# Fifteen pairs of a Strassen feed-forward block: seven wide quarter products into two-bank accumulators

## The chip, the cores and the metric

The kernel runs on one core of a Trainium2 chip. The core has a matrix engine (TensorE; PE in the profile, with its weight loads as PEld), a vector engine (VectorE, DVE), a scalar engine (ScalarE, ACT), GpSimd (POOL) and SyncE (SP), which here only issues DMAs. Each engine works through its own queue in order. TensorE writes its results to an accumulator memory, PSUM, of eight banks; one bank holds 512 float32 values in each of 128 partitions. The metric is the device time of one execution in microseconds (us), lower is better.

## The reference, cut to what matters

One layer of a streaming encoder: a feed-forward half step, a mixer of convolution and gated linear attention, a second feed-forward half step, an embedding gate, a final norm. 512 tokens, model width 1024, feed-forward width 2816, all in float32.

```python
def _swiglu(x, w_in, w_out):
    gate, up = jnp.split(x @ w_in, 2, axis=-1)
    return (jax.nn.silu(gate) * up) @ w_out
...
        h = h + 0.5 * _swiglu(_rmsnorm(h, ffn1_norm[i]), ffn1_w_in[i], ffn1_w_out[i])
        z = _rmsnorm(h, mix_norm[i]) @ w_in[i]
...
        h = h + jnp.concatenate([y_conv, y_gla], axis=-1) @ w_out[i]
        h = h + 0.5 * _swiglu(_rmsnorm(h, ffn2_norm[i]), ffn2_w_in[i], ffn2_w_out[i])
        gate = jax.nn.sigmoid(_rmsnorm(h, ple_norm[i]) @ ple_w_gate[i])
        h = h + gate * (p[i] @ ple_w_proj[i])
    return _rmsnorm(h, final_norm)
```

## The kernel before

Activations lie transposed: features on the 128 partitions, the 512 tokens along the free axis. Every operand of TensorE is split into a high and a low part (ACT rounds the high part, DVE subtracts it from the original to get the low part), and a product is the sum of three: high by high, high by low, low by high.

The first product of each feed-forward block is done in eleven **pairs**: pair i takes 256 gate columns and the 256 matching up columns of w_in. A pair is a 2 by 2 block product in the form of Strassen and Winograd: seven quarter products in place of eight. `m1` to `m7` in `ffn` are the seven; each multiplies a quarter of the weights (512 by 256, named a11, a12, a22, s1 to s4) with a quarter of the activations (512 by 256 tokens, b11, b21, b22, t1 to t4). A few pairs at the start (pairs 0 and 1 in the first block, pair 0 in the second) are done plainly, without the seven products.

There are two forms of a quarter product, both over four blocks of 128 rows and two blocks of 128 columns:

- `mul` (line 341): for each row and column block three matrix instructions of 256 columns, 24 in all, into one bank (two halves of 256).
- `mul2` (line 357): for each row and column block one instruction of 512 columns, which takes the weight's high part against the high and the low half of the activations side by side, and then one of 256 columns for the weight's low part: 8 and 8, 16 in all, into two banks (a tile `pd`). The sum of the two 256-column halves is left to DVE.

Before the change m7 and m4 use `mul2`; m1, m2, m6, m5 and m3 use `mul`. One accumulator, p.x, is shared by m1, m6, m5 and m3, and ACT copies its state out (`snap`) after each of the first three; p.y holds m2; p.w holds m7 and m4. `plus` (line 687) adds an accumulator and a copy on DVE and multiplies by the row scale.

The second product (by w_out) runs in pieces of 48 instructions for a group of two pairs (`second`, line 822); a piece writes two banks, and DVE adds them to the residual h. Two pieces come with each pair. The list `units` sets the order on TensorE; in a steady stretch it is m6, m7, m5 of pair i, m1, m2 of pair i+1, a piece, m4, m3 of pair i, a piece. `drive` makes the weights' parts four units ahead of their use (`AHEAD`), fetches seven to nine ahead, and runs what a unit leaves over (`left`) around the next unit. The wrapper `Ordered` pins the order of PE, DVE and ACT to the order in which the program issues.

Weights come in 512 KB transfers on SP's queue into six raw buffers (`wr`); the high and low parts have six buffers each (`wh`, `wl`).

PSUM before: five single banks and one `aux` bank in a pool that is open all the time, and two more banks that are either one two-bank tile (`bank2`, p.w) or two single banks (`spare`).

After the second block comes the embedding gate stage (from line 1610), one Strassen product of its own, whose order on ACT and DVE is mostly left to the scheduler.

Of the kernel before, what the change touches and what calls it, by code (L numbers as in the profile page):

```python
# [62 lines left out]
def block_kernel(ctx: ExitStack, tc: tile.TileContext, a: dict, out: bass.AP):  # L63
# [12 lines left out]
    pp = ctx.enter_context(tc.tile_pool(name="ps", bufs=8, space=PSUM))  # L76
# [30 lines left out]
    wide, turn_no, narrow_only = [None, None], [0], [True]  # L107

    def region(double):
        if wide[0] != double:  # L110
            if wide[1] is not None:
                wide[1].close()
            wide[:] = double, ExitStack()
            wide.append(wide[1].enter_context(tc.tile_pool(name=nm("pw"), bufs=1, space=PSUM)))
        return wide[-1]

    def bank2():
        return region(True).tile([P, 2, SEQ], F32, tag="mm2", bufs=1, name=nm("pd"))

    def spare():  # L120
        return region(False).tile([P, SEQ], F32, tag="mm", bufs=2, name=nm("ps"))

    def bank():
        turn_no[0] += 1
        if not narrow_only[0] and turn_no[0] % 7 in (5, 6):
            return spare()
        return pp.tile([P, SEQ], F32, tag="mm", bufs=5, name=nm("ps"))

    def aux():
        return pp.tile([P, SEQ], F32, tag="aux", bufs=1, name=nm("ax"))  # L130

# [187 lines left out]
    class Norm:  # L319
# [5 lines left out]
        def add(self, h):  # L325
            if self.n == 0:
                act.activation(self.acc, h, AF.Square)
            else:
                sq = tmp("sq", bufs=3)
# [11 lines left out]
    def mul(ps, w, x, first, last, ks=range(4)):  # L341

        (wh, wl), k0 = w, ks[0]
        for k in ks:
            xh, xl = x[k]
# [11 lines left out]
    def mul2(ps, w, x, first, last):  # L357

        wh, wl = w
        at = [(k, i, slice(i * P, (i + 1) * P)) for k in range(4) for i in range(2)]  # L360
        for k, i, cs in at:
            pe.matmul(two(ps[:, i]), wh[:, k, cs], x[k][0], start=(first and k == 0), stop=False, skip_group_check=True)
        for k, i, cs in at:
            pe.matmul(ps[:, i, 0:HALF], wl[:, k, cs], x[k][1], start=False, stop=last and k == 3, skip_group_check=True)
# [6 lines left out]
    class Right:  # L371
# [3 lines left out]
        def __init__(self, rows, gname):  # L375
            self.rows, self.gname = rows, gname
            self.raw, self.op = {}, {}
            for k in range(2):
                for half in range(2):
                    hs = slice(half * HALF, (half + 1) * HALF)  # L380
                    self.op[f"b{k + 1}{half + 1}"] = [tuple(t[:, hs] for t in rows[4 * k + c]) for c in range(4)]
# [20 lines left out]
        def split(self, *names):  # L402
            for name in names:
                op = self.op[name] = []
                for jp in range(2):
                    src = self.raw.pop((*T_KEYS[name], jp))
                    if name == "t4":
                        for jj in range(2):
                            hi, lo = self.op["b12"][2 * jp + jj]
                            act.copy(hi, src[:, jj])  # L410
                            sub(lo, src[:, jj], hi.bitcast(F32))
                            op.append((whole_of[id(self.rows[2 * jp + jj][0])][1][:, :, HALF:], hi))
# [5 lines left out]
                    if name == "t3":  # L418
                        whole = whole_of[id(pair_[0])][1]
                        op += [(whole[:, :, jj * HALF:(jj + 1) * HALF], hi[:, jj]) for jj in range(2)]  # L420
                    else:
                        op += [(hi[:, jj], lo[:, jj]) for jj in range(2)]
# [100 lines left out]
    def square_x(i):  # L523

        tile_, t0, nt = squares[i]
        sq = tmp("sq", bufs=3).rearrange("p (t c) -> p t c", t=nt)
# [55 lines left out]
    ps0 = [bank(), bank(), spare(), spare()]  # L582
# [79 lines left out]
    def ffn(w_in, w_out, x, gname, given, first, rsb, hooks, plain, far={}, casts={}, adds=()):  # L662
# [9 lines left out]
        pairs = {i: given.get(i) or Left(w_in, 2 * i) for i in range(npair)}  # L672

# [13 lines left out]
        def plus(ps, t, i, name):  # L687
            o = tmp(name)
            if len(ps.shape) == 3:
# [17 lines left out]
        def snap(ps, name, **kw):  # L707
            o = tmp(name, **kw)
# [13 lines left out]
        def m1(p):  # L722
            p.x = bank()
            mul(p.x, p.part("a11"), x.op["b11"], True, False)
            p.a = snap(p.x, "sq", bufs=3)

        def m2(p):
            p.y = bank()
            mul(p.y, p.part("a12"), x.op["b21"], True, True)
# [4 lines left out]
            if p is pairs[start]:  # L734
                after["m7" if plain else "m5", start] = [gate0] if plain else [lambda: pairs[start + 1].cast("s1", "s3"), gate0]
                return []
            return [gate0]

        def m6(p):
            mul(p.x, p.part("s2"), x.op["t2"], False, False)  # L740
            p.u2 = snap(p.x, "u2", bufs=1)

        def m7(p):
            p.w = bank2()
            mul2(p.w, p.part("s3"), x.op["t3"], True, False)

        def m5(p):
            mul(p.x, p.part("s1"), x.op["t1"], False, False)
            p.u = plus(p.w, snap(p.x, "sq", bufs=3), 1, "u1")
# [13 lines left out]
        def plain_unit(j):  # L763

            up, i, k = j // 4, j // 2 % 2, j % 2
            def run(p):
                if not j:
                    p.g, p.s = {}, {}
                if not k:
                    p.x = bank()  # L770
# [53 lines left out]
        def second(cut):  # L824
# [7 lines left out]
            def piece(n, g, begin, final, key=None):  # L832
# [7 lines left out]
                def run():  # L840
                    left = []
                    wh, wl = got.pop((f0, n, g))
                    for i in range(2):
                        if begin:
                            ps[n + i] = (spare if last and n == 4 else bank)()
# [6 lines left out]
                        if final:  # L852
                            h = hT[n + i]
                            dve.scalar_tensor_tensor(out=h, in0=ps[n + i], scalar=0.5, in1=h,
                                                     op0=ALU.mult, op1=ALU.add)
                            if last:
                                hi, lo = bt2(s="hg")
                                act.activation(hi, h, AF.Copy, scale=vec(gname, n + i))
                                left.append((h, hi, lo, vec(gname, n + i)))
# [42 lines left out]
        for i in range(start, npair):  # L902
            add("m6", i)
# [5 lines left out]
            else:  # L909
# [26 lines left out]
        narrow_only[0], turn_no[0] = False, 0  # L936
# [17 lines left out]
    hooks.update({("m5", 3): lambda *_: made[0](), ("m5", 4): lambda *_: constants(),  # L954
# [288 lines left out]
    def outputs(t2):  # L1243
# [13 lines left out]
        for t in (2 * t2, 2 * t2 + 1):  # L1257
            junk = tmp("sq", bufs=3)
# [239 lines left out]
    narrow_only[0] = True  # L1498

    def plain_block(p, up, i, mid={}):  # L1500
        ps = (spare if i else bank)()
# [34 lines left out]
    hooks.update({("m7", 10): lambda *_: turn_p(0), ("m5", 10): lambda *_: turn_p(1)})  # L1536
# [129 lines left out]
    def inputs(t, e, spare=False):  # L1666
# [3 lines left out]
        pq, pt = bank(), aux() if spare else bank()  # L1670
# [89 lines left out]
    def kept(ps, name, **kw):  # L1760
        o = tmp(name, **kw)
# [16 lines left out]
    x_, y_ = [bank(), bank()], [bank(), bank()]  # L1778
# [8 lines left out]
    m1 = [kept(p_, "sq", bufs=3) for p_ in x_]  # L1787
# [24 lines left out]
    w_ = [bank(), bank()]  # L1812
# [9 lines left out]
    x5 = [kept(p_, "sq", bufs=3) for p_ in x_]  # L1822
# [7 lines left out]
    b22 = [added(high(t)) for t in q22]  # L1830
# [36 lines left out]
    wide[1].close()  # L1867
# [23 lines left out]
```

## Time and profile before

| | |
|---|---|
| Time, median of 3 runs | 941.72 us (941.43 to 942.06) |
| The profiled execution | 941.44 us |
| Its span, first to last instruction | 939.7 us |
| VectorE busy, share of the span | 785.9 us, 84% |
| ScalarE busy | 483.1 us, 51% |
| GpSimd busy | 55.9 us, 6% |
| Granted TensorE clock, mean | 0.997 |

A row of the profile gives an engine, an operation, output and inputs by the program's tile names, a count, the busy time and the mean duration. Nearly all instructions are recorded through one helper, so their line is always L46, and one tells them apart by tiles: `hg` are the normalized activations, `t` their sums, `act` the input of the second product, `wr` raw weights, `wh` and `wl` their parts, `ps` single banks, `pd` two-bank tiles, `sq` and `u` the copies of accumulators, `g` a gate value, `h` the residual.

### The profile page before, as it was taken

How to read it: one execution, taken by the hardware profiler on the slowest of the kernel's cores; microseconds unless marked ns; L12 is line 12 of the kernel's file. 1: busy time of each engine (PE TensorE's matmuls, PEld its weight loads, DVE VectorE, ACT ScalarE, POOL GpSimd, SP SyncE). 2: the span in 40 equal slices, each digit the busy share in tenths (PEclk: the TensorE clock that was granted, in tenths of full speed). 3: DMA queues.
4: the chain of work that ended last, by engine and by line, in shares of the span. 5: the costliest groups of instructions: out<-in, count | busy, mean ns of one | idle time of the engine just before them, and what ended most of it. 6: DMA issues, size and time to landing. Idle time of an engine off the chain costs nothing.

```text
span 939.7 us, 14172 instructions
## 1 busy us (share of the span) xinstructions
PE 929.2 (99%) x5611; PEld 816.8 (87%) x5611; DVE 785.9 (84%) x1077; ACT 483.1 (51%) x730; POOL 55.9 (6%) x74
## 2 busy tenths in 40 slices
PE   9999999999999999999999999999999999999996
PEld 7898999899989988788877889999899999998875
DVE  6798987898789676999986789988888888876986
ACT  5874444344444474463564875444434433446873
POOL 0100000000000111001120020000000000000130
PEclk9999999999999999999999999999999999999998
DMA  7633332342223593256552563432243224347463
GB/s 228 189 107 114 113 107 88 101 135 90 90 91 112 147 261 86 68 126 144 136 134 75 150 150 97 132 104 79 91 135 112 68 90 135 105 160 208 90 109 115
DMA packets 108134, 114.45 MB, mean 122 GB/s; under 512 B 5203, under 2 KB 96517, under 8 KB 108068
## 3 DMA queue, kind: packets, MB, share of 16 engines
q1 hardware_dynamic: 101748, 94.67, 32.8%
q0 software_dynamic: 6304, 18.88, 11.0%
q8 instruction: 44, 0.72, 0.3%
q14 instruction: 22, 0.18, 0.1%
q10 hardware_dynamic: 16, 0.00, 0.0%
HBM read 93.61 MB, written 2.10 MB: 102 GB/s over the span
## 4 chain that ended last, share of the span: by engine, by line
PE 97%; DMA 1%; ACT 1%; DVE 1%; issue 0%; POOLq 0%; ACTq 0%; DVEq 0%
PE ps L46 84%; PE pd L46 11%; PE ax L46 1%; DMA sm<-in_ple_w_gate 1%; ACT s L46 0%; DVE s L46 0%; ACT wh L46 0%; ACT wl L46 0%; ACT sq L46 0%; DVE u L46 0%; DVE rs L46 0%; ACT yc L46 0%; DVE y L46 0%; DVE g L46 0%; DVE lnsq L46 0%
## 5 line engine op out<-in xcount | busy, mean ns | idle before, releaser
L46 PE MATMUL ps<-hg,wh 128*128 128x256 f32 (+1 forms) x1232 | 262.2, 312 | 0.1
L46 DVE TENSOR_TENSOR wl<-wr,wh 128x1024 fp32r<-128x1024 f32 (+2 forms) x161 | 188.1, 1179 | 37.7 <-ACT wh L46 37.6
L46 PEld LDWEIGHTS ps<-hg,wh 128*128 128x128 f32 x1232 | 201.7, 191 | 14.1 <-issue 1.3
L46 ACT CAST wh<-wr 128x1024 fp32r<-128x1024 f32 (+2 forms) x178 | 177.6, 1020 | 50.1 <-DMA wr<-in_ffn_w_out 27.4
L46 PE MATMUL ps<-hg,wl 128*128 128x256 f32 (+1 forms) x616 | 187.6, 311 | 0.0
L46 PE MATMUL ps<-act,wh 128*128 128x512 f32 x512 | 158.0, 390 | 0.0
L46 ACT ACTIVATE s<-g 128x512 f32<-128x512 f32 x48 | 30.4, 633 | 191.2 <-DVE g L46 191.2
L46 PEld LDWEIGHTS ps<-hg,wl 128*128 128x128 f32 x616 | 117.6, 191 | 6.4
L46 PEld LDWEIGHTS ps<-act,wh 128*128 128x128 f32 x512 | 95.1, 188 | 19.0
L46 PE MATMUL ps<-t,wh 128*128 128x256 f32 x608 | 111.0, 283 | 0.0
L46 PE MATMUL ps<-act,wl 128*128 128x512 f32 x256 | 99.6, 389 | 0.0
L46 PEld LDWEIGHTS ps<-t,wh 128*128 128x128 f32 x608 | 95.9, 192 | 1.2
L46 PE MATMUL ps<-t,wl 128*128 128x256 f32 x304 | 86.1, 283 | 0.0
L46 DVE SCALAR_TENSOR_TENSOR cv<-glu,cw,cv 128x502 f32<-128x502 f32 (+24 forms) x90 | 61.8, 729 | 0.3
L46 DVE TENSOR_TENSOR wl<-sm,wh 128x1024 fp32r<-128x1024 f32 x42 | 51.2, 1221 | 8.8 <-ACT wh L46 8.8
L46 PEld LDWEIGHTS ps<-t,wl 128*128 128x128 f32 x304 | 58.3, 192 | 0.0
L46 PEld LDWEIGHTS ps<-act,wl 128*128 128x128 f32 x256 | 48.1, 188 | 10.1
L46 PE MATMUL ps<-wh,hg 128*128 128x512 f32 x176 | 54.8, 393 | 0.1
L46 DVE SCALAR_TENSOR_TENSOR h<-ps,h 128x512 f32<-128x512 f32 x80 | 51.7, 682 | 2.3 <-PE ps L46 2.2
L46 ACT COPY sq<-ps 128x512 f32<-128x512 f32 x42 | 24.4, 584 | 55.9 <-PE ps L46 55.7
L46 ACT CAST wh<-sm 128x1024 fp32r<-128x1024 f32 x42 | 43.8, 1043 | 5.3 <-DMA sm<-in_ple_w_gate 2.9
L46 DVE TENSOR_TENSOR u<-pd,u 128x512 f32<-128x512 f32 x57 | 39.3, 689 | 5.9 <-PE pd L46 4.6
(307 smaller groups left out, 1501.5 us busy)
## 6 DMA issues: line engine op xcount, KB each, us to landing
wr<-in_ffn_w_in SPq DMA_DIRECT2D x84, 512.0 KB
wr<-in_ffn_w_out SPq DMA_DIRECT2D x32, 512.0 KB
wr<-in_w_in SPq DMA_DIRECT2D x20, 512.0 KB
wl<-wr POOLq DMA_DIRECT2D x18, 512.0 KB, 5.3
wr<-in_ffn_w_out SPq DMA_DIRECT2D x16, 384.0 KB
wr<-in_w_out SPq DMA_DIRECT2D x8, 512.0 KB
wq<-in_ple_w_gate SPq DMA_DIRECT2D x8, 512.0 KB
wl<-wq POOLq DMA_DIRECT2D x8, 512.0 KB, 4.9
```

Source lines behind the costliest of these rows:

```text
L46: inst = call(*args, **kwargs)
```

## The change

All later pairs (from the second pair after the first Strassen pair on: pairs 4 to 10 of the first block, 3 to 10 of the second, fifteen in all) do all seven products with `mul2` into two-bank accumulators. What follows from that is changed along with it.

- PSUM is laid out per stage. Two banks (`fixed`) are always open. With them goes either `singles` (three banks and `aux`, and two banks that are `spare` or one `double(True)`), or, while `mode` is 2, `doubles` (two two-bank tiles for p.x and p.y, and one for p.w).
- p.x and p.y are two-bank tiles; which of the two is taken first alternates from pair to pair, so that m1 writes the one that held p.y of the pair before.
- The pairs come one behind the other: m1, m2, m6, m7, m5, piece, m4, m3, piece, all of pair i. The pieces write the two `fixed` banks.
- ACT copies 1024 values a partition instead of 512 out of p.x (two buffers `sq` of 1024 in place of three of 512). `plus` on a two-bank tile and a two-bank copy adds 1024 values, then the two halves, then multiplies by the row scale. m3's result is copied by halves and summed.
- The gate after m2 is summed behind m7 and goes through silu behind m5; m3's silu runs ahead of the piece behind it.
- In the last group, pieces n = 2 and 4 write two-bank tiles, and their two additions to h wait for both products.
- In the embedding gate stage the accumulators are `spare` and `fixed` banks, and the rounding of q22 is put behind the copies `x5`.

```diff
+    def fixed():
+        return psum(region("fixed"), 2, [P, SEQ])
...
+    def double(last=False):
+        kind = ("fixed", "doubles" if mode[0] == 2 else "singles", "double")
+        return psum(region(*kind) if last else region(*kind[:2]), 1 if last else 2, [P, 2, SEQ])
...
     def mul2(ps, w, x, first, last):
+        if len(ps.shape) == 2:
+            return mul(ps, w, x, first, last)
...
-            pe.matmul(two(ps[:, i]), wh[:, k, cs], x[k][0], start=(first and k == 0), stop=False, skip_group_check=True)
+            pe.matmul(two(ps[:, i]), wh[:, k, cs], x[k][2], start=(first and k == 0), stop=False, skip_group_check=True)
...
+        for i, p in pairs.items():
+            p.wide = start + 2 <= i
...
         def plus(ps, t, i, name):
...
             else:
-                dve.tensor_tensor(out=o, in0=ps, in1=t, op=ALU.add)
+                dve.tensor_tensor(out=t, in0=ps, in1=t, op=ALU.add)
+                dve.tensor_tensor(out=two(o), in0=t[:, :, 0:HALF], in1=t[:, :, HALF:], op=ALU.add)
...
         def m1(p):
-            p.x = bank()
-            mul(p.x, p.part("a11"), x.op["b11"], True, False)
-            p.a = snap(p.x, "sq", bufs=3)
+            mode[0] = 2 if p.wide else 1
+            if p.wide and (p.f % 4 or p is pairs[end]):
+                p.y = double()
+            p.x = double() if p.wide else bank()
+            mul2(p.x, p.part("a11"), x.op["b11"], True, False)
+            p.a = p.both = snap(p.x, "sq")
...
         def m3(p):
-            mul(p.x, p.part("s4"), x.op["b22"], False, True)
-            s = silu(times_row(p.x, 1, "g1"))
+            mul2(p.x, p.part("s4"), x.op["b22"], False, True)
+            if p.wide:
+                o = tmp("g1")
+                act.copy(two(o), p.x[:, :, 0:HALF])
+                dve.tensor_tensor(out=two(o), in0=p.x[:, :, HALF:], in1=two(o), op=ALU.add)
+                dve.tensor_tensor(out=two(o), in0=two(o), in1=row(1), op=ALU.mult)
...
         for i in range(start, npair):
+            add("m1", i)
+            add("m2", i)
             add("m6", i)
             add("m7", i)
             add("m5", i)
             if i == end:
                 half, rest = second(cut_of[i])
                 units.append(half[0])
-            else:
-                add("m1", i + 1)
-            add("m2", i + 1)
+            elif i == start and not plain:
+                add("m2", i + 1)
             units += due[:1]
+            if i == start:
+                add("m2", i + 1)
             add("m4", i)
             add("m3", i)
...
-    x_, y_ = [bank(), bank()], [bank(), bank()]
+    mode[0] = 1
+    x_, y_ = [spare(), spare()], [fixed(), fixed()]
...
-    b22 = [added(high(t)) for t in q22]
+    b22 = [added(later_high(t)) for t in q22]
```

More of the change, by code (lines that the diff above doesn't have):

```diff
@@ L105, in tmp, with close_to, region, psum @@
         return tp.tile([P, w], dt, tag=s, bufs=bufs, name=nm(s))
[L107 to L118, printed above, removed]
-    def spare():
[L121 to L127, printed above, removed]
+    def close_to(n):
+        while len(stack) > n:
+            stack.pop()[1].close()
+    def region(*names):
+        for level, name in enumerate(names):
+            if len(stack) <= level or stack[level][0] != name:
+                close_to(level)
+                es = ExitStack()
+                stack.append((name, es, es.enter_context(tc.tile_pool(name=nm("p" + name), bufs=1, space=PSUM))))
+        return stack[len(names) - 1][2]
+    def psum(pool_, n, shape, tag="mm"):
+        return pool_.tile(shape, F32, tag=tag, bufs=n, name=nm("pd" if len(shape) == 3 else "ps"))
+    def bank():
+        if mode[0] == 0:
+            turn_no[0] += 1
+            at = turn_no[0] % 7
+            if at in (3, 4):
+                return fixed()
+            if at in (5, 6):
+                return spare()
+        return psum(region("fixed", "singles"), 3, [P, SEQ])
+    def fixed():
+        return psum(region("fixed"), 2, [P, SEQ])
+    def spare():
+        return psum(region("fixed", "singles", "spare"), 2, [P, SEQ])
+    def double(last=False):
+        kind = ("fixed", "doubles" if mode[0] == 2 else "singles", "double")
+        return psum(region(*kind) if last else region(*kind[:2]), 1 if last else 2, [P, 2, SEQ])
     def aux():
-        return pp.tile([P, SEQ], F32, tag="aux", bufs=1, name=nm("ax"))
+        if mode[0] == 2:
+            return fixed()
+        return psum(region("fixed", "singles"), 1, [P, SEQ], "aux")
     zeros = cp.tile([P, P], F32, name="zeros")
@@ L344, in mul @@
         for k in ks:
[L345 removed]
+            xh, xl = x[k][:2]
             for i in range(2):
@@ L380, in __init__ @@
                     hs = slice(half * HALF, (half + 1) * HALF)
-                    self.op[f"b{k + 1}{half + 1}"] = [tuple(t[:, hs] for t in rows[4 * k + c]) for c in range(4)]
+                    self.op[f"b{k + 1}{half + 1}"] = [
+                        (*(t[:, hs] for t in rows[4 * k + c]), whole_of[id(rows[4 * k + c][0])][1][:, :, hs])
+                        for c in range(4)]
         def pieces(self, k, jp):
@@ L581, in block_kernel @@
     warm_up(4)
-    ps0 = [bank(), bank(), spare(), spare()]
+    ps0 = [fixed(), fixed(), spare(), spare()]
     split_w(0, 1, dve.tensor_copy, 2)
@@ L705, in gated_block, with snap @@
             dve.tensor_tensor(out=p.m[:, i], in0=u, in1=s, op=ALU.mult)
-        def snap(ps, name, **kw):
-            o = tmp(name, **kw)
+        def snap(ps, name, rest=None):
+            if name == "sq":
+                o = rest if rest is not None else two(tmp(name, 2 * SEQ))
+                if len(ps.shape) == 2 and rest is None:
+                    act.copy(o[:, 0], ps)
+                else:
+                    act.copy(o, ps)
+                return o
+            o = tmp(name, bufs=1)
             act.copy(o, ps)
@@ L722, in m1 @@
         def m1(p):
-            p.x = bank()
-            mul(p.x, p.part("a11"), x.op["b11"], True, False)
-            p.a = snap(p.x, "sq", bufs=3)
+            mode[0] = 2 if p.wide else 1
[4 more added lines that the diff above has]
+            p.a = p.both = snap(p.x, "sq")
+            if not p.wide:
+                p.a = p.both[:, 0]
         def m2(p):
-            p.y = bank()
-            mul(p.y, p.part("a12"), x.op["b21"], True, True)
+            if not (p.wide and (p.f % 4 or p is pairs[end])):
+                p.y = double() if p.wide else (fixed if p is pairs[start + 1] and not plain else bank)()
+            mul2(p.y, p.part("a12"), x.op["b21"], True, True)
             def gate0():
@@ L755, in m3, with gate1 @@
         def m3(p):
-            mul(p.x, p.part("s4"), x.op["b22"], False, True)
-            s = silu(times_row(p.x, 1, "g1"))
+            mul2(p.x, p.part("s4"), x.op["b22"], False, True)
+            if p.wide:
+                o = tmp("g1")
+                act.copy(two(o), p.x[:, :, 0:HALF])
+                dve.tensor_tensor(out=two(o), in0=p.x[:, :, HALF:], in1=two(o), op=ALU.add)
+                dve.tensor_tensor(out=two(o), in0=two(o), in1=row(1), op=ALU.mult)
+                if p is not pairs[end]:
+                    after["m6", p.f // 2 + 1] = [lambda: act_parts(p)]
+                def gate1():
+                    p.s1 = silu(o)
+                return [gate1, lambda: gated(p, p.s1, p.u, 1)] + ([lambda: act_parts(p)] if p is pairs[end] else [])
+            elif p is pairs[start] and not plain:
+                o = times_row(p.x, 1, "g1")
+                after["m6", p.f // 2 + 1] = [lambda: gated(p, silu(o), p.u, 1), lambda: act_parts(p)]
+                return []
+            else:
+                s = silu(times_row(p.x, 1, "g1"))
             if p is pairs[end]:
@@ L769, in run @@
                 if not k:
-                    p.x = bank()
+                    p.x = (fixed if j == 6 else bank)()
                 ps = p.x
@@ L842, in run, with products @@
                     wh, wl = got.pop((f0, n, g))
-                    for i in range(2):
-                        if begin:
-                            ps[n + i] = (spare if last and n == 4 else bank)()
+                    if begin and last and n in (2, 4):
+                        t = double(n == 4)
+                        ps[n], ps[n + 1] = t[:, 0], t[:, 1]
+                    elif begin:
+                        ps[n], ps[n + 1] = fixed(), fixed()
+                    def products(i):
                         cs = slice(i * P, (i + 1) * P)
@@ L851, in run, with add_to @@
                                 k == 0, k == kn - 1)
[L852 to L859, printed above, removed]
+                    def add_to(i):
+                        h = hT[n + i]
+                        dve.scalar_tensor_tensor(out=h, in0=ps[n + i], scalar=0.5, in1=h,
+                                                 op0=ALU.mult, op1=ALU.add)
+                        if last:
+                            hi, lo = bt2(s="hg")
+                            act.activation(hi, h, AF.Copy, scale=vec(gname, n + i))
+                            left.append((h, hi, lo, vec(gname, n + i)))
+                    for i in range(2):
+                        products(i)
+                        if final and not (last and n in (2, 4)):
+                            add_to(i)
+                    if final and last and n in (2, 4):
+                        add_to(0)
+                        add_to(1)
                     if key:
@@ L1496, in block_kernel @@
     hg = nhg
-    narrow_only[0] = True
+    mode[0] = 1
     def plain_block(p, up, i, mid={}):
-        ps = (spare if i else bank)()
+        ps = (fixed if i else spare)()
         cs = slice(i * P, (i + 1) * P)
@@ L1811, in block_kernel @@
         act.copy(both[:, i], x_[i])
-    w_ = [bank(), bank()]
+    w_ = [fixed(), fixed()]
     times(w_, s3_, b3, first=True)
@@ L1821, in block_kernel @@
     b4 = [low(later_high(t)) for t in t2]
-    x5 = [kept(p_, "sq", bufs=3) for p_ in x_]
+    x5 = [kept(p_, "sq") for p_ in x_]
+    squared = act.latest
     i2 = inputs(2, 1)
```

60 lines of the change are left out of this document (33 added, 27 removed).

## The prediction

> **What bounds the kernel now.** I read the page first, then the waits of TensorE, then the chain of waits.
>
> ```profile
> span 939.7 us, 14172 instructions
> PE 929.2 (99%) x5611; PEld 816.8 (87%) x5611; DVE 785.9 (84%) x1077; ACT 483.1 (51%) x730; POOL 55.9 (6%) x74
> PE 97%; DMA 1%; ACT 1%; DVE 1%; issue 0%; POOLq 0%; ACTq 0%; DVEq 0%
> PE ps L46 <- DVE zeros L46: 1.1, 1, 1.1
> PE ps L46 <- DVE s L46: 0.8, 1, 0.8
> PE ps L46 <- ACT yc L46: 0.2, 1, 0.2
> ```
>
> TensorE is busy for 929.2 of 939.7 us, 97% of the chain is its own, and the last three rows are all its waits: 2.1 us. So time goes only if TensorE's stream gets shorter; DVE at 84% is the next engine. The chain of waits through the steady stretch shows one period:
>
> ```profile
> 248.49 2.79 PE pd L46 x16
> 251.28 14.11 PE ps L46 x96
> 265.39 2.77 PE pd L46 x16
> 268.15 11.22 PE ps L46 x72
> 279.37 2.79 PE pd L46 x16
> ```
>
> From one m7 (`pd`, 16 instructions) to the next is 279.37 - 248.49 = 30.88 us: m7 2.79; m5, m1, m2 and a piece, 96 instructions, 14.11; m4 2.77; m3, a piece and the next m6, 11.22. Nothing is idle in it.
>
> **Removed from TensorE.** The timeline of TensorE gives the price of an instruction by its width:
>
> ```profile
> 251.12 0.40 PE L46 MATMUL ps<-t,wh 128*128 128x256 f32 x2
> ...
> 259.76 0.63 PE L46 MATMUL ps<-act,wh 128*128 128x512 f32 x2
> ...
> 265.22 1.98 PE L46 MATMUL pd<-hg,wh 128*128 128x512 f32 x8
> 267.04 1.11 PE L46 MATMUL pd<-hg,wl 128*128 128x256 f32 x8
> 267.99 0.40 PE L46 MATMUL ps<-hg,wh 128*128 128x256 f32 x2
> ```
>
> The 72 instructions of 256 columns from 251.12 to 259.76 take 8.64 us, 0.120 each; the 24 of 512 up to 265.22 take 5.46, 0.2275 each. Twice 0.120 is 0.240, so each merged pair saves 12 ns: the fixed part of an instruction. A `mul` is 24 x 0.120 = 2.88 us. A `mul2` is 1.82 + 0.95 = 2.77 behind a piece, and 2.79 behind a 256-column instruction (m7 above). Five products of a wide pair change form: m1 follows a piece, the other four a product, so 5 x 2.88 - (2.77 + 4 x 2.79) = 0.47 us. Fifteen pairs: **7.0 us**. The new period is 30.88 - 0.47 = 30.41 us. The column count stays (6144 a product); only 8 instructions of 24 go.
>
> The Trainium skill speaks against this size: its page "TensorE: Matmul & The Clock Gate", section "Back-to-back issue gap", gives a warm instruction N/2.4 + 2.5 ns, so the fixed part is 2.5 ns. By it 15 x 5 x 8 instructions would give back an estimated 1.5 us. The rows here have 0.120 us where it has 0.109, and this case's trace does not agree.
>
> **Added to DVE.** Here lies the danger. The timeline of DVE in the same stretch (in brackets, idle time before a row):
>
> ```profile
> 249.66 1.29 DVE L46 TENSOR_TENSOR act<-m,act 128x512 fp32r<-128x512 f32 x2 [2.02 <-ACT act L46]
> ...
> 254.81 0.69 DVE L46 TENSOR_TENSOR u<-pd,sq 128x512 f32<-128x512 f32 x1 [0.45 <-ACT sq L46]
> 255.54 0.69 DVE L46 TENSOR_TENSOR u<-pd,u 128x512 f32<-128x512 f32 x1
> 256.26 0.69 DVE L46 TENSOR_TENSOR u<-u,bc 128x512 f32<-128x512 f32 x1
> 256.88 1.22 DVE L46 TENSOR_TENSOR sm<-wr,wr 128x1024 f32<-128x1024 f32 x1
> 258.13 1.23 DVE L46 TENSOR_TENSOR sm<-sm,wr 128x1024 f32<-128x1024 f32 x1
> 259.27 1.22 DVE L46 TENSOR_TENSOR wl<-wr,wh 128x1024 fp32r<-128x1024 f32 x1
> ...
> 263.81 0.68 DVE L46 TENSOR_TENSOR g<-ps,sq 128x512 f32<-128x512 f32 x1
> 264.53 0.69 DVE L46 TENSOR_TENSOR g<-g,bc 128x512 f32<-128x512 f32 x1
> 265.14 1.28 DVE L46 SCALAR_TENSOR_TENSOR h<-ps,h 128x512 f32<-128x512 f32 x2
> 266.86 1.23 DVE L46 TENSOR_TENSOR wl<-sm,wh 128x1024 fp32r<-128x1024 f32 x1 [0.44 <-ACT wh L46]
> ...
> 274.23 1.23 DVE L46 TENSOR_TENSOR wl<-wr,wh 128x1024 fp32r<-128x1024 f32 x1 [1.64 <-ACT wh L46]
> ...
> 280.55 1.29 DVE L46 TENSOR_TENSOR actL<-m,actH 128x512 fp32r<-128x512 f32 x2 [2.15 <-ACT actH L46]
> ```
>
> By start to start, 1024 values cost 1.14 us (258.13 to 259.27), 1.25 if the next one needs them (256.88 to 258.13); 512 values cost 0.72 if the next one needs them (254.81 to 255.54), about 0.61 if not (264.53 to 265.14). From 249.66 to 280.55 DVE waits 0.45 + 0.44 + 1.64 + 2.15 = 4.7 us, so its work is 30.89 - 4.7 = 26.2 us a pair. The change adds, per wide pair: a 1024-value addition ahead of the gate's two steps, +1.25; in each of the two `u` sums 1.25 in place of one 0.72, +0.53 twice; an addition ahead of m3's row scale, +0.72. That is 3.0 us, and **DVE's work becomes 29.2 us in a period of 30.41**. No row has DVE reading two banks at once: the nearest are 1.14 (1024 values from SBUF, 258.13) and two rows of 512 from PSUM at 0.64 each (265.14, two in 1.28); I take 1.14, since 512 from PSUM (0.68) costs what 512 from SBUF (0.69) costs. With 1.28 the work is 29.6. Other ends: below 26.2 it can't go, as nothing leaves DVE; for a cost like two dependent instructions, 1.44, it is 30.1.
>
> The 4.7 us are not lost to the new order: they are places where DVE had run ahead and stood for ACT, which stood for TensorE. So DVE may now fall behind TensorE by some us, and what counts is whether anything is late then. I lay its queue out in its new order, time zero at m1: m2 ends at 5.6, m6 8.35, m7 11.1, m5 13.9, piece 19.4, m4 22.1, m3 24.9, second piece 30.4. ACT's part comes from these groups:
>
> ```profile
> L46 ACT COPY sq<-ps 128x512 f32<-128x512 f32 x42 | 24.4, 584 | 55.9 <-PE ps L46 55.7
> L46 ACT CAST wh<-wr 128x1024 fp32r<-128x1024 f32 x159 | 163.1, 1047 | 45.0 <-DMA wr<-in_ffn_w_out 27.4 <-PE ps L46 6.4 <-issue 4.9
> L46 ACT CAST act<-m 128x512 fp32r<-128x512 f32 x32 | 18.4, 622 | 5.5 <-DVE m L46 5.3
> ```
>
> A copy of 512 costs 0.58 us and a rounding of 1024 1.05, so a copy of 1024 about 1.0; three of these and m3's copy add some 1.8 us to ACT, which is busy 51%: hidden. The low parts of `act` stand first in the tail of m6: 8.35 + 1.0 (copy) + two roundings and the last 0.6 = 11.4. Behind it DVE has s4's low part (12.5), gate sum (15.1), a piece's weights (16.3), `u` behind m5 (18.9), a11's part and two sums (22.3), two `h` additions (23.6), a12's part and a sum (25.9), `u` and `m` behind m4 (29.2), s2's part (30.3), m3's sum and scale (31.7), two parts (33.9), `h` and `m` (35.8): 5.4 us behind the pair's end. The next pair's first jobs (3.4) end at 39.2, ahead of its `act` at 41.8 (30.4 + 11.4, the first of two at 40.6). So DVE still rests about 1.2 us a pair, and the lag does not grow.
>
> With this lag the handovers are: p.w read first at 17.5, m4 writes it from 19.4; the `fixed` banks free at 22.9, wanted at 24.9; p.x free at 31.0, wanted as the next p.y by m2 at 33.2; `act` at 11.4, wanted by the piece from 13.9, its last pair from 15.3. **All are met with about 2 us.** If DVE's cost grows past that, the cover is gone and TensorE waits at these places. Only pair 10 breaks the alternation: its m1 writes the bank of pair 9's p.x, wanted at 30.4, free at 31.0: 0.7 us with the signal, in each block, 1.4. The last pairs have no further weights to make, so the lag dissolves there.
>
> **Moved.** The pairs' order takes the piece from 11 to 5.6 us behind m6; SP's fetches, with the same distance in units, keep six raw buffers for six loads a pair; they are freed later by DVE's lag, but a22's, freed at 9.2, is wanted again as raw data only at 18.9. These edits and the layouts cost nothing in the steady pairs. At the starts DVE is fuller (busy time per stretch is the third engine's number):
>
> ```profile
> 98.90:130.20 31.30, 31.30 (x204) 28.58 (x204) 28.38 (x34) 12.72 (x17) 0.00 (x0) 1.00 0.33 102
> 254.10:285.00 30.90, 30.90 (x202) 28.34 (x201) 25.98 (x31) 12.68 (x16) 0.00 (x0) 1.00 0.34 103
> 587.00:617.90 30.90, 30.90 (x203) 28.34 (x202) 27.84 (x34) 15.79 (x21) 0.00 (x0) 1.00 0.33 103
> ```
>
> 28.4 and 27.8 us of DVE against 26.0 in the steady stretch: the last narrow pairs enter the wide ones with a lag, and there the banks change layout. Bounds: 0 to 3 us a block; I take 0.3 each. In the last stage two roundings of q22 stand ahead of the copies `x5`:
>
> ```profile
> 907.84 1.05 ACT L46 CAST wh<-wq 128x1024 fp32r<-128x1024 f32 x1
> 909.79 1.04 ACT L46 CAST wh<-wq 128x1024 fp32r<-128x1024 f32 x1
> ```
>
> They move behind; TensorE's one wait near there is 0.8 us (for `s`, above), so 0 to 0.8 can come back, or go if `s` comes later; I take 0.3.
>
> **Sum.** 941.44 (profiled) - 7.0 + 1.4 + 0.6 - 0.3 = 936.1; the median lies 0.28 above the profiled run: **936.4 us**.
>
> **Rivals.** (1) The handovers are missed a little: with 1.44 for the two-bank sums DVE has 0.3 us of rest, and 0.2 to 0.3 us a pair is lost; 15 x 0.25 = 3.8 gives 940.2. For it: margins of 2 us against a lag of 5.4; against it: 1024 values cost less than twice 512 in every row. (2) Slower: **DVE becomes the bound**. It decides from 30.88 us of DVE work a pair, 4.7 more than now where I count 3.0; if waits for ACT's longer copies in DVE's queue stay at about half of the old 4.7, a pair takes 29.2 + 2.3 = 31.5, and 15 x (31.5 - 30.88) + 2.0 gives 953. For it: `act` now has one product less of cover; against it: DVE lags, and a lagging engine finds its inputs ready. (3) The merged instruction saves little because the fixed part isn't per instruction, or a pair isn't wide at all: 941 to 942. Against it stand m7 and m4, which already have this form at 2.77 and 2.79. The page's rule named above belongs here, with its estimated 1.5 us. (4) No stall at all and the full tail: 941.7 - 7.0 - 0.8 = 933.9 or a little less.
>
> **Chances.** Forecast, 934 to 938.5: 0.62. (1) 938.5 to 941.7: 0.13, half of it within 0.2%. (2) 0.14. (3) 0.05. (4) 0.06. A measurement can tell about 0.2%, 1.9 us. Faster 0.62 + 0.06 + 0.07 = 0.75, same 0.06 + 0.05 = 0.11, slower 0.14. The range 933.8 to 941.8 leaves out (2) and some of (4).
>
> **What would show it.** Right: 75 products of 16 instructions, so 600 fewer on TensorE; 2.77 to 2.79 us for each; a steady period near 30.4; DVE near 29 of it, with 1 us idle; one short wait at m1 of pair 10. Wrong: TensorE waiting for `u`, `g` or `h` of DVE in every pair, or a DVE without idle time and a period above 30.9.

## The result, and the profile after

| | before | after |
|---|---|---|
| Median of 4 runs each | 941.58 us (941.43 to 942.06) | 935.09 us (934.88 to 935.23) |
| The profiled execution | 941.44 us | 935.23 us |
| Its span | 939.7 us | 933.4 us |

After over before is 0.993, with a 95% interval of 0.9918 to 0.9943: 6.5 us less, against 5.3 us forecast.

The page of after, its rows of engines and the shares of the chain (busy time, share of the span, instructions):

```profile
span 933.4 us, 12982 instructions
PE 923.0 (99%) x5011; PEld 785.5 (84%) x5011; DVE 826.7 (89%) x1107; ACT 510.0 (55%) x745; POOL 57.0 (6%) x74
PE 97%; DVE 2%; issue 0%; ACT 0%; POOLq 0%; DVEq 0%
L46 ACT COPY sq<-pd 128x1024 f32<-128x1024 f32 x45 | 45.8, 1017 | 87.8 <-PE pd L46 50.4
L46 DVE TENSOR_TENSOR sq<-pd,sq 128x1024 f32<-128x1024 f32 x45 | 54.8, 1218 | 0.8 <-PE pd L46 0.8
```

TensorE has 5611 - 5011 = 600 instructions fewer, and its busy time falls by 6.2 us, nearly the whole gain (the span falls by 6.3). DVE's work grows by 40.8 us, to 89%, and the time still falls. The last two rows are the new two-bank work, 45 times each (three a pair): ACT's copy of 1024 values takes 1.02 us and DVE's addition 1.22, as assumed.

The waits of TensorE in after (total us, times, longest):

```profile
PE ps L46 <- DVE zeros L46: 1.1, 1, 1.1
PE pd L46 <- DVE g L46: 0.9, 1, 0.9
PE ps L46 <- ACT yc L46: 0.2, 1, 0.2
```

The first and the last stood there before. The wait for `s` in the last stage is gone, and one for `g` is new. The chain of waits of after through the steady stretch (start, length, engine, tile, instructions):

```profile
238.50 13.94 PE pd L46 x80
252.44 5.47 PE ps L46 x24
257.90 5.56 PE pd L46 x32
263.46 5.47 PE ps L46 x24
268.93 13.94 PE pd L46 x80
...
299.37 13.94 PE pd L46 x80
```

A row of 80 is m1, m2, m6, m7 and m5 of one pair, five products of 16 instructions: 13.94 us, 2.79 each. A pair takes 268.93 - 238.50 = 30.43 us and the next one 30.44; before it was 30.88. No time is idle in it. So a wide pair saves 0.45 us. DVE's timeline of after over the same pair (in brackets, the idle time before a row):

```profile
248.45 1.29 DVE L46 TENSOR_TENSOR act<-m,act 128x512 fp32r<-128x512 f32 x2 [1.18 <-ACT act L46]
249.92 1.23 DVE L46 TENSOR_TENSOR wl<-wr,wh 128x1024 fp32r<-128x1024 f32 x1 [0.17 <-ACT wh L46]
...
254.79 1.22 DVE L46 TENSOR_TENSOR sq<-pd,sq 128x1024 f32<-128x1024 f32 x1
256.04 0.69 DVE L46 TENSOR_TENSOR u<-sq 128x512 f32<-128x512 f32 x1
...
260.90 1.28 DVE L46 SCALAR_TENSOR_TENSOR h<-ps,h 128x512 f32<-128x512 f32 x2
...
268.82 0.68 DVE L46 TENSOR_TENSOR g<-pd,g 128x512 f32<-128x512 f32 x1
...
278.89 1.29 DVE L46 TENSOR_TENSOR actL<-m,actH 128x512 fp32r<-128x512 f32 x2 [1.18 <-ACT actH L46]
...
299.25 0.68 DVE L46 TENSOR_TENSOR g<-pd,g 128x512 f32<-128x512 f32 x1
```

DVE now stands idle for 1.18 + 0.17 = 1.35 us a pair, where it stood for 4.7, and 30.43 - 1.35 = 29.1 us is work. Its first read of p.w, which comes behind m5, ends at 256.0, 17.5 us after the pair's start at 238.50; the two additions to h end at 262.18, 23.7 after it. The sum of m3, the last reader of p.x, ends at 269.5: 0.6 us into the next pair, and it holds nobody up, since that bank is next written by m2.

Where the 6.3 us of span came from, by the times of the same four instructions in both traces (the start of the first three, the end of the last):

| Stretch | before | after | difference |
|---|---|---|---|
| Start of the span to m7 of the first pair | 64.97 | 65.35 | +0.38 |
| From there to the first weights of the mixer | 289.14 | 286.05 | -3.09 |
| Mixer and start of block 2, to its first m7 | 212.85 | 212.84 | 0.0 |
| From there to the last instruction on `act` | 309.26 | 307.07 | -2.19 |
| Rest, with the embedding gate stage | 63.51 | 62.12 | -1.39 |

Block 1 has seven wide pairs, and 7 x 0.45 = 3.15 us is what it gains. Block 2 has eight, which would be 3.6; 1.4 of it is lost. The last stage gains more than forecast. The 0.38 us at the start come from the first matmuls, four of which took 1.66 us in place of 1.19 in this execution; the change doesn't touch them, and in the trace of aux_x2 below that m7 starts at 64.80.

### The profile page after: what moved, and what is told of

The parts are those of the page before. It is cut to its first block, busy times and chain, and to the rows that moved or that the text cites. A ratio compares the mean times of both kernels' runs of the same rounds, so it can differ in the third digit from the quotient of the medians.

```text
span 933.4 us, 12982 instructions
## 1 busy us (share of the span) xinstructions
PE 923.0 (99%) x5011; PEld 785.5 (84%) x5011; DVE 826.7 (89%) x1107; ACT 510.0 (55%) x745; POOL 57.0 (6%) x74
## 4 chain that ended last, share of the span: by engine, by line
PE 97%; DVE 2%; issue 0%; ACT 0%; POOLq 0%; DVEq 0%
PE ps L46 60%; PE pd L46 37%; DVE wl L46 1%; DVE u L46 0%; DVE sm L46 0%; DVE g L46 0%; DVE h L46 0%; DVE wr L46 0%; DVE rs L46 0%; ACT yc L46 0%; DVE y L46 0%; DVE s L46 0%; DVE lnsq L46 0%; POOLq L1965 0%; DVE ms L46 0%
## 5 line engine op out<-in xcount | busy, mean ns | idle before, releaser
L46 PE MATMUL ps<-hg,wh 128*128 128x512 f32 (+1 forms) x512 | 131.5, 353 | 0.0
L46 PE MATMUL pd<-hg,wh 128*128 128x512 f32 x512 | 127.6, 391 | 0.9 <-DVE g L46 0.9
L46 PEld LDWEIGHTS pd<-hg,wh 128*128 128x128 f32 x512 | 93.9, 188 | 19.8 <-issue 1.3
L46 PEld LDWEIGHTS ps<-hg,wh 128*128 128x128 f32 x512 | 89.8, 190 | 14.1 <-issue 1.3
L46 PE MATMUL pd<-t,wh 128*128 128x512 f32 x392 | 98.3, 393 | 0.0
L46 PE MATMUL ps<-hg,wl 128*128 128x512 f32 (+1 forms) x256 | 85.6, 350 | 0.0
L46 PEld LDWEIGHTS pd<-t,wh 128*128 128x128 f32 x392 | 70.5, 189 | 12.6
L46 PEld LDWEIGHTS pd<-hg,wl 128*128 128x128 f32 x512 | 69.8, 190 | 5.0
L46 PE MATMUL pd<-hg,wl 128*128 128x256 f32 x512 | 71.4, 282 | 0.0
L46 DVE TENSOR_TENSOR sq<-pd,sq 128x1024 f32<-128x1024 f32 x45 | 54.8, 1218 | 0.8 <-PE pd L46 0.8
```

The lines of the kernel that those rows point to most:

```text
L46: inst = call(*args, **kwargs)
```

## The experiments

My theory was that each instruction left out on TensorE saves its fixed part, about 12 ns, that this is the whole gain, and that DVE has a margin of about 1.3 us a pair. Its rivals: the gain comes from the new order or the new tail; the fixed part is much smaller; DVE's margin is larger or smaller than its idle time shows. The kernel before ran beside each of them, with medians of 941.5 to 941.7 us, so times of different runs are set against each other directly.

**split_wide** issues the 512-column instruction of `mul2` as two of 256, everything else as after.

```diff
-            pe.matmul(two(ps[:, i]), wh[:, k, cs], x[k][2], start=(first and k == 0), stop=False, skip_group_check=True)
+            pe.matmul(ps[:, i, 0:HALF], wh[:, k, cs], x[k][0], start=(first and k == 0), stop=False, skip_group_check=True)
+            pe.matmul(ps[:, i, HALF:], wh[:, k, cs], x[k][1], start=False, stop=False, skip_group_check=True)
```

> The changed kernel, but every instruction of 512 columns in a two-bank product is issued as two of 256 (same accumulators, same order, same work on VectorE and ScalarE). 113 products have this form (7 in each of 15 wide pairs, 2 in each of 4 narrow ones). Theory (a fixed 12 ns per instruction): a product goes from 2.79 back to 2.88 us, 113 x 0.09 = 10.2 us more, about 945.3 us. Rival (fixed part 2.5 ns as the Trainium skill's page has it): 113 x 8 x 2.5 ns = 2.3 us more, 937.4. Rival (the gain came from order or layout): 935.1.

Measured: 944.93 us against 941.72 before, ratio 1.0035 (1.0021 to 1.0048). The chain of waits of split_wide:

```profile
241.48 14.39 PE pd L46 x120
255.87 5.47 PE ps L46 x24
261.34 5.75 PE pd L46 x48
267.09 5.47 PE ps L46 x24
272.56 14.39 PE pd L46 x120
```

The five products take 14.39 us with 120 instructions where after takes 13.94 with 80, and a pair takes 31.08. In the whole run 904 more instructions cost 944.93 - 935.09 = 9.8 us, 10.9 ns each; in the steady pair, 0.65 us for 56, it is 11.6. So the gain is the number of instructions. Each matrix instruction here brings a weight load of its own (5011 of both in the page of after), so the 11 ns are the price of the two together; no run takes them apart. All the rest of the change, with split instructions, is 3.2 us slower than before, since m7 and m4 lose there what they had: 19 pairs with 16 instructions more each, 304 x 10.9 ns = 3.3 us.

**end_wide** and **seven_wide** do two pairs (the last of each block) and seven wide, with the order and the banks of after. The edit, 6 standing for seven_wide:

```diff
-            p.wide = start + 2 <= i
+            p.wide = i == end
```

```diff
-            p.wide = start + 2 <= i
+            p.wide = start + 6 <= i
```

> The changed kernel with the last pair of each block wide and all others narrow: the new order and layouts, 2 wide pairs in place of 15. Theory (the order costs nothing in the steady pairs, whose period was 30.89 us in the run with no wide pair, and the change of layout was what that run lost at the blocks' ends): 935.1 + 13 x 0.45 = 940.9, up to 1 us more for the change of layout ahead of the last pair. Rival (the order with narrow pairs costs, and only the wide form makes up for it): 944 to 947.

> The changed kernel with seven wide pairs in place of fifteen (the last three of the first block, the last four of the second). Theory (0.45 us for each wide pair): 935.1 + 8 x 0.45 = 938.7 us. Rival (the gain sits in order or layout, or a change of layout in mid-block costs): off that line by over 1 us.

Measured: end_wide 941.21 us against 941.5, ratio 0.9996 (0.9987 to 1.0005); seven_wide 938.6 against 941.65, ratio 0.9968 (0.9956 to 0.998). The chain of waits of end_wide, m7 of three narrow pairs in the new order:

```profile
186.70 2.79 PE pd L46 x16
...
217.59 2.79 PE pd L46 x16
...
248.48 2.79 PE pd L46 x16
```

The period is 30.89 us, that of before: the order of pairs and the later pieces cost and gain nothing there. Its one new wait is 1.1 us for `u`, in block 2. From 2 to 7 wide pairs the time falls by 2.6 us, 0.52 a pair, and from 7 to 15 by 3.5, 0.44 a pair. The traces show it by blocks, with the bounds of the table above: block 1 takes 288.77, 287.82 and 286.05 us with one, three and seven wide pairs, 0.4, 1.3 and 3.1 less than before, so the gain there is close to linear in the pairs. Block 2 loses 1.4 to 1.6 us against such a line in all three kernels, however many of its pairs are wide.

**none_wide** has no wide pair; so that the two-bank pieces of the last group still find their tiles, the layout changes ahead of that group's second piece.

```diff
-            p.wide = start + 2 <= i
+            p.wide = False
...
+                        mode[0] = 2
```

> The changed kernel with no wide pair: all order, layout and last-stage edits stay, the 75 products go back to 24 instructions in one bank. Theory (only the form pays in the pairs, and the last stage's order 1.4 us): 935.1 + 15 x 0.45 minus at most 0.9 for the wait at the first wide pair, 940.9 to 941.9 less nothing else, so near 940.9. Rival (the pairs' order or the layouts cost or gain on their own): above 942.5 or below 939.5.

Measured: 947.53 us, ratio 1.0061 (1.0048 to 1.0075), 6.6 more than expected. Its steady period is 30.89 too (m7 at 155.73 and at 186.62); the loss lies where the layout now changes. TensorE's timeline of none_wide at the end of block 1:

```profile
325.31 0.28 PE L46 MATMUL ps<-hg,wl 128*128 128x256 f32 x1
327.97 0.50 PE L46 MATMUL pd<-actH,wh 128*128 128x512 f32 x1 [2.38 <-DVE g L46]
```

and the stretch from that instruction on (PE, PEld, DVE, ACT, POOL busy with counts, granted clock, DMA share, GB/s):

```profile
327.97:332.20 4.23, 4.23 (x12) 3.33 (x13) 2.18 (x4) 2.60 (x5) 0.00 (x0) 0.60 1.06 208
```

The first tile of the new layout waits 2.38 us for the last reader of the old one, `g`, and in the 4.2 us behind it the granted clock is 0.60 on average. Block 2 has the same wait at 854.94 (1.55 us) and one of 1.1 for `u`, and the last stage has one of 0.7 for a DMA. By its time alone this run speaks for the rival; by its trace it says nothing against the theory of the period, and shows the price of a change of layout in a place where its last reader is late.

**dve_plus1** and **dve_plus3** repeat the gate's half-sum in each wide pair once or three times; the repeats compute the same values.

```diff
-                dve.tensor_tensor(out=two(o), in0=t[:, :, 0:HALF], in1=t[:, :, HALF:], op=ALU.add)
+                for _ in range(2 if name == "g1" else 1):
+                    dve.tensor_tensor(out=two(o), in0=t[:, :, 0:HALF], in1=t[:, :, HALF:], op=ALU.add)
```

> The changed kernel, the gate's addition of two halves (512 values, SBUF) done once more in each wide pair, with the same result: about 0.65 to 0.72 us more VectorE work a pair. The trace of the changed kernel has it idle for 1.35 us of a period of 30.44. Theory (TensorE is still the bound, VectorE has 1.35 us to spare): 935.1 to 935.8 us. Rival (VectorE's lag already sets the pairs): 15 x 0.7 = 10 us more, 945.

> The same, the addition done three times more: 2.0 to 2.1 us more VectorE work a pair. Theory (1.35 us to spare, then VectorE is the bound): 0.65 to 0.75 us over, 15 pairs, 10 to 11 us more, about 945.5 us, with TensorE waiting for VectorE in every wide pair. Rival (the idle time is longer when it is needed, since VectorE stands for ScalarE): 935 to 937.

Measured: dve_plus1 (range of 2) 937.54 us against 941.65, ratio 0.9958 (0.9944 to 0.9972); dve_plus3 (range of 4) 948.13, ratio 1.007 (1.0056 to 1.0084), 2.6 us more than expected. DVE's timeline of dve_plus1 in a steady pair:

```profile
248.15 1.29 DVE L46 TENSOR_TENSOR act<-m,act 128x512 fp32r<-128x512 f32 x2 [0.47 <-ACT act L46]
249.61 1.23 DVE L46 TENSOR_TENSOR wl<-wr,wh 128x1024 fp32r<-128x1024 f32 x1 [0.17 <-ACT wh L46]
```

One more addition takes 0.71 us of DVE's idle time and leaves 0.64; TensorE waits nowhere in these pairs. All the same the run is 2.4 us slower than after, where at most 0.7 was expected. By the bounds of the table, block 1 takes 1.4 us more, the mixer 1.1 and block 2 0.3: waits of 0.2 to 0.7 us each, from start to start, at the ends of the blocks and the start of the mixer. The list of waits has three of them, for `act` and `hg`; I read them as DVE's lag, which has to be worked off there, so that the margin is used up in these places before it is in the steady pairs. Three more additions are too much. The chain of waits of dve_plus3, one row a pair:

```profile
198.62 5.86 PE pd L46 x32
...
229.69 5.86 PE pd L46 x32
...
260.75 5.86 PE pd L46 x32
```

and its waits of TensorE:

```profile
PE pd L46 <- DVE sq L46: 7.3, 15, 1.5
```

The period is 31.07, 0.63 above after's, and DVE's idle time is gone: DVE has become the bound. By the sum it should be 29.1 + 3 x 0.7 = 31.2 us of work. It is m4 (the start of each row of 32) that waits, for DVE's first read of p.w. The list counts idle time only, 0.34 us for each of thirteen pairs, where the period grows by 0.63; thirteen such pairs give 8.2 of the 13 us. The two longest waits, 1.4 and 1.5 us in the last pair of each block, cost 1.7 each from start to start, and waits for `act` at the end of block 1 another 1.1. So DVE sets the steady pairs from about 1.3 us of work a pair above what the change has. Where the whole gain is gone no run shows; going back from dve_plus3, which is 6.5 us slower than before, at 15 us of time for 1 us of work a pair, it is an estimated 1.7 us above.

**tail_only** and **no_tail** take the change of the last stage by itself: the roundings of q22 behind the copies `x5`, put into the kernel before, and taken out of after.

```diff
+    squared = act.latest
...
-    b22 = [added(high(t)) for t in q22]
+    b22 = [added(later_high(t)) for t in q22]
```

> The kernel before with one edit: the rounding of q22 in the last stage stands behind the copies x5. Theory (the last stage's 1.4 us came from this order): 941.6 - 1.4 = 940.2 us. Rival (they came from the new banks there): 941.6.

> The changed kernel without that edit: the rounding of q22 may again stand ahead of the copies x5. Theory: 935.1 + 1.4 = 936.5 us, with TensorE waiting for s near the end again. Rival (banks, not order): 935.1.

Measured: tail_only 940.58 us against 941.72, ratio 0.999 (0.9981 to 0.9999); no_tail 935.28, ratio 0.9933 (0.9921 to 0.9946). ACT's timeline of no_tail in the last stage:

```profile
902.74 1.05 ACT L46 CAST wh<-wq 128x1024 fp32r<-128x1024 f32 x1
904.21 0.58 ACT L46 COPY sq<-ps 128x512 f32<-128x512 f32 x1
904.69 1.05 ACT L46 CAST wh<-wq 128x1024 fp32r<-128x1024 f32 x1
905.64 0.59 ACT L46 COPY sq<-ps 128x512 f32<-128x512 f32 x1
```

The roundings stand among the copies again, and yet TensorE waits for nothing there: the stage takes 62.16 us, with the edit 62.12. In the kernel before the same edit brings 0.8 of the stage's 63.5. So the 1.4 us that after gains in this stage are there without the moved rounding too; beside the other edits it is worth nothing that can be measured. Nor do they come from the wide pairs: with two and with seven of them the stage takes 62.2 us. The accumulators in other banks are left as the likeliest cause, but this was not tried by itself, and the change also touches the buffers of `sq` in this stage and the point ahead of it at which p is transposed.

**aux_x2** and **later_a12** go for the one new wait, 0.91 us at m1 of pair 3 of block 2. TensorE's timeline of after there, and DVE's:

```profile
603.62 0.39 PE L46 MATMUL ps<-act,wl 128*128 128x512 f32 x1
604.92 2.08 PE L46 MATMUL pd<-hg,wh 128*128 128x512 f32 x8 [0.91 <-DVE g L46]
```

```profile
601.82 1.22 DVE L46 TENSOR_TENSOR wl<-sm,wh 128x1024 fp32r<-128x1024 f32 x1
602.96 1.22 DVE L46 TENSOR_TENSOR wl<-wr,wh 128x1024 fp32r<-128x1024 f32 x1
604.09 0.68 DVE L46 TENSOR_TENSOR g<-ps,bc 128x512 f32<-128x512 f32 x1
```

The sum of m3 of pair 2 reads p.x of that pair (`ps`) until 604.8, behind two parts of weights, and m1 of pair 3 is the first to write the new layout. The listed 0.91 us are idle time; from start to start m1 comes 1.30 us behind the instruction ahead of it where 0.23 is usual, so 1.07 are lost. aux_x2 puts that p.x into another of the old single banks; later_a12 makes one of the two parts a unit later.

```diff
-            p.x = double() if p.wide else bank()
+            p.x = double() if p.wide else (aux if p is pairs[start + 1] and not plain else bank)()
```

```diff
-    hg, norm = ffn(ffn2_in, ... ("m1", 3): 3, ("m2", 3): 3}, ...)
+    hg, norm = ffn(ffn2_in, ... ("m1", 3): 3, ("m2", 3): 2}, ...)
```

> The changed kernel, p.x of the last narrow pair of the second block in the aux bank, so that m1 of the first wide pair writes banks that are free. Theory (the one wait of TensorE for VectorE, 0.9 us, with the ramp behind it 1.1): 934.0 to 934.2 us. Rival (another handover of VectorE's lag takes its place): 935.1.

> The changed kernel, the low part of a12 of the first wide pair of the second block made one unit later, so that VectorE takes the last narrow pair's gate (g) 1.14 us earlier. With p.x of that pair in the aux bank the wait of 0.9 us at m1 of the first wide pair had stayed. Theory (the new bank layout waits for the last reader of the whole old layout, wherever it lies, and that is g): the wait goes, 935.1 - 1.0 = 934.1 us. Rival (the wait passes to a later step of VectorE's lag): 935.1.

Measured: aux_x2 935.11 us against 941.65, ratio 0.993 (0.9918 to 0.9943); later_a12 934.78 against 941.5, ratio 0.9928 (0.9915 to 0.9942). TensorE's waits, first of aux_x2 and then of later_a12:

```profile
PE pd L46 <- DVE g L46: 0.9, 1, 0.9
```

```profile
PE pd L46 <- ACT wh L46: 0.5, 1, 0.5
```

The other bank changes nothing, so moving that one tile is not enough. That the new layout waits for every reader of the old one fits this; that the other bank lies under the same new tile would fit it too, and the two were not told apart. With the weights' part moved the wait for `g` is gone, and m2 of the same pair waits 0.46 us at 607.20 for that part instead: half the wait comes back in the trace (block 2 takes 306.61 in place of 307.07), but the runs of later_a12 (933.95 to 935.28) and of after can't be told apart.

## Why the prediction was right, step by step

The forecast of 936.4 was 1.3 us too high: the mechanism was right, and four terms of the sum were off, in both directions, by 0.3 to 1.4 us each. That misses of 3.6 us in all come to no more than 1.3 is luck.

- **Form, 7.0 us: right.** 600 instructions went, a merged product takes 2.79 us, and the period is 30.43 where 30.41 was worked out. Measured are 0.45 a pair, 6.7 in all. By split_wide the fixed part is 10.9 to 11.6 ns, where I took 12. The rival by which the merged instruction saves little is refuted by that run. The Trainium skill's 2.5 ns ("TensorE: Matmul & The Clock Gate", section "Back-to-back issue gap", where it is the gap of an isolated instruction, without its weight load) does not agree with it; by it split_wide would have cost an estimated 2.3 us and not 9.8.
- **DVE, 29.2 us of 30.41: right**, at 29.1 of 30.43, and so was the choice to price two banks read at once like 1024 values from SBUF, at 1.14 us or 1.25 with an instruction behind it that needs them: the trace has 1.25 (254.79 to 256.04). The queue laid out by hand put the first read of p.w at 17.5 and the end of the additions to h at 23.6, and the trace has 17.5 and 23.7. The handovers are met, and rival (1) didn't come.
- **DVE as the bound (rival 2): didn't come, and its point is about right: slower than before from 30.88 us of work.** dve_plus3 lies beyond it, at a period of 31.07, and is 6.5 us slower than before; 15 x (31.07 - 30.88) would be 2.9. The estimate above, 29.1 + 1.7, puts the point at 30.8. What I hadn't seen is that part of the gain goes earlier, at the ends of the blocks, with 29.8 us of work (dve_plus1).
- **A wait of 0.7 us at m1 of pair 10 in each block, 1.4 us: wrong.** The failed step is "its m1 writes the bank of pair 9's p.x". The chain above has m1 of pair 10 of block 1 start at 299.37 directly behind the piece, while DVE begins to read pair 9's p.x at 299.25 and is at it until 299.9. So it writes another tile. I had taken the order of the program's allocations for a fixed alternation; why the allocator gave it the other tile no run shows.
- **Starts of the wide pairs, 0.3 us each: mis-sized.** Block 1 lost nothing, block 2 some 1.4 us, nearly 1.1 of it at the wait for `g` (0.91 idle) and the rest in gaps of about 0.1 beside it and in the pair before. Together 1.4 for the 0.6 taken, within the bounds given.
- **Last stage, 0.3 us: mis-sized, and its reason wrong.** It gained 1.4 us. "They move behind" is worth about 1 us in the kernel before, as tail_only shows, but nothing in after, as no_tail shows; I had costed all other edits of the stage, the banks among them, at nothing. Nor do both roundings stand ahead of the copies in the kernel before: by its rows the second, at 909.79, follows the first copy.

By the span, the terms as measured: -6.7 (form), 0 (pair 10), +1.4 (starts), -1.4 (last stage), +0.4 (the first matmuls), together -6.3, which is the difference of the two spans. That it comes out is no proof of the terms, since the starts are taken as what block 2 fell short of its eight pairs.

## What to carry to other kernels

Where TensorE bounds a kernel, count its instructions as well as its columns: two narrow products with the same weights can go as one wide instruction into two halves of a bank that lie side by side, and each instruction saved is worth its fixed part (11 ns here). The price is an accumulator of twice the size, and it falls on the engine that reads it; add its work up per period, with the idle time of before taken as slack if it stands for an engine that is itself ahead, and look at the ends of the stage first, where the lag has to be worked off. A change of PSUM layout waited here for a late reader of the old one (0.91, 1.55 and 2.38 us), so put it where that reader is early, and follow which tile the allocator really gives before charging a wait to one.

## What the runs showed of the hardware

A pause of TensorE cost more than itself in one place here. TensorE's timeline of none_wide behind its pause of 2.38 us (which ends at 327.97), and behind the one of 1.55 us in block 2:

```profile
328.54 0.44 PE L46 MATMUL pd<-actH,wl 128*128 128x512 f32 x1
328.78 0.63 PE L46 MATMUL pd<-actH,wh 128*128 128x512 f32 x1
329.20 0.63 PE L46 MATMUL pd<-actL,wh 128*128 128x512 f32 x1
...
332.18 0.40 PE L46 MATMUL pd<-actH,wl 128*128 128x512 f32 x1
332.41 0.40 PE L46 MATMUL pd<-actH,wh 128*128 128x512 f32 x1
...
854.94 0.50 PE L46 MATMUL pd<-actH,wh 128*128 128x512 f32 x1 [1.55 <-DVE g L46]
855.28 0.40 PE L46 MATMUL pd<-actL,wh 128*128 128x512 f32 x1
855.51 0.39 PE L46 MATMUL pd<-actH,wl 128*128 128x512 f32 x1
```

After the longer pause the first instructions still run at full rate, 0.24 us start to start; from 328.78 to 332.18 there are eight that take 3.40 us, 0.425 each, and then it is 0.23 again. These eight cost 8 x 0.2 = 1.6 us beside the 2.38. After the shorter pause the rate is full from the start (855.28 to 855.51). The granted clock of none_wide, by stretches of 3.41 us (columns as above), drops to half here:

```profile
325.34:328.75 3.41, 1.03 (x6) 0.71 (x5) 1.83 (x3) 1.78 (x4) 1.75 (x2) 1.00 0.96 161
328.75:332.16 3.41, 3.41 (x9) 2.65 (x8) 2.14 (x3) 1.78 (x4) 0.00 (x0) 0.50 1.07 221
```

That is where the 0.60 above comes from. In the stretch ahead of it TensorE was busy for 1.03 us of 3.41.

The Trainium skill's page "TensorE: Matmul & The Clock Gate", section "What's actually happening", has the clock halved after an idle window of about 3.4 us, on windows that run free. The trace agrees with the halved rate and with the 3.4 us for which it lasted, and the half rate begins 0.78 us behind the end of the pause, which fits windows that run free; but 2.38 us of idleness, not 3.4, were enough. One such pause was seen, so from what length on it happens, and how far it depends on where the pause lies, stays open. The four runs of none_wide lie 2.6 us apart and those of after 0.35, so it need not have come in each of them.
